# First modulation rows of a transformer layer: fp32 products replaced by split single-pass products with a folding matmul

## The chip, the cores and the metric

The kernel runs on one core of a Trainium2 chip. The time is the device time of one execution in microseconds (us). The engines are TensorE (PE, matmuls; its weight loads are shown apart as PEld), VectorE (DVE), ScalarE (ACT), GpSimd (POOL) and SyncE (SP), whose queue issues the DMA transfers. Each engine works through its instructions in order; semaphores tie them together.

## The reference

One layer of a diffusion backbone works on 1024 latent tokens and 256 context tokens of width 1024. At its start two vectors, `c` for the latent tokens and `c_ctx` for the context tokens, go through silu and a weight matrix of 1024 x 6144. The six pieces of the result shift, scale and gate the tokens later on. The change concerns the first two pieces, shift and scale of the first norm:

```python
mod = jax.nn.silu(c) @ w_mod[l] + b_mod[l]
mod_c = jax.nn.silu(c_ctx)[None, :] @ w_mod[l] + b_mod[l]
sh1, sc1, g1, sh2, sc2, g2 = jnp.split(mod, 6, axis=-1)
sh1c, sc1c, g1c, sh2c, sc2c, g2c = jnp.split(mod_c, 6, axis=-1)
...
h = modulate(rms_norm(x, norm1_w[l]), sh1, sc1)
hc = modulate(rms_norm(ctx, norm1_w[l]), sh1c, sc1c)
```

`h` and `hc` then enter a combined input projection, two token mixers (windowed attention with context keys, and a two-way mLSTM), the merge, and a convolutional feed-forward part. All data is fp32.

## The kernel before

The tokens stand in blocks of 128. Most large products are done in split form: an fp32 operand is taken apart into a high part, which ACT writes as `fp32r` (a format that PE multiplies in a single pass), and a low part, the difference, which DVE writes. The helper is `split_from` (lines 47 to 49); `mm3` (lines 85 to 92) adds up three of the four products of the parts.

`stage_startup` (from line 276) makes the first modulation rows. The silu of both vectors is `sil`, 128 x 8 x 2: for each of 8 blocks `k` of the inner dimension a stationary operand of two columns, one for each vector. The weights come as 16 blocks `wm` of 128 x 1024 (512 KB), 8 for each of two sweeps `i`; a sweep yields half of the channels of shift and scale. For each block two fp32 matmuls of 512 columns add into two PSUM tiles `pm`, of which two partitions are in use (lines 359 to 365). After a sweep, `modulation(i)` (line 320) copies the two rows into `mrow` on DVE and ACT, turns them by 8 transposes into `pmT`, so that channels lie along partitions, and DVE makes `mods` out of that.

With `mods` ACT shifts and scales the turned context (`xct`, line 348) into `hfc` (line 337), and splits it into `hcH` and `hcL`. The first half of the channels is done after sweep 0, the second after sweep 1. The context's keys (`pkc`), values (`pvc`) and mLSTM inputs (`cx`) follow as split products, with the latent tokens' norms, transposes and modulation (`hf`, `hH`, `hL`) in between; from about 106 us on the kernel runs on PE in split products.

The order on each engine is not the order of the code: a scheduler places the instructions, and what is printed below for the order is what comes out of it. The weights of the start share one pool of 11 blocks (`block`, line 285) with the context and latent tokens and the weights `w1b` that follow; a load into a block waits for the last reader of what lay there. SP issues all these loads in one fixed order. The tiles `hT` (8 pairs of `hH` and `hL`, 128 x 1024 each) are first written when the latent tokens are modulated, long after the two sweeps.

Of the kernel before, what the change touches and what calls it, by code (L numbers as in the profile page):

```python
# [8 lines left out]
F32 = mybir.dt.float32  # L9
F32R = mybir.dt.float32r  # L10
AF = mybir.ActivationFunctionType
ALU = mybir.AluOpType
# [4 lines left out]
P = 128  # L17
# [4 lines left out]
KT = D // P  # L22
# [20 lines left out]
def copy_act(nc, out, in_, scale=1.0):  # L43
    nc.scalar.activation(out, in_, AF.Copy, scale=scale)  # L44


def split_from(nc, hi, lo, src, eng="v"):
    copy_act(nc, hi, src)
    (nc.vector if eng == "v" else nc.gpsimd).tensor_tensor(lo, src, hi.bitcast(F32), op=ALU.subtract)  # L49
# [50 lines left out]
def layer_kernel(ctx: ExitStack, tc: tile.TileContext, A: dict, out: bass.AP, dbg=None):  # L100
# [58 lines left out]
    with ExitStack() as st:  # L159
        at = attention_setup(E, st)  # L160
        stage_startup(E, at)
        if "hT" in dbg:
            for k in range(KT):
                nc.sync.dma_start(dbg["hT"][0, k * P : (k + 1) * P], hH[k].bitcast(F32))
                nc.sync.dma_start(dbg["hT"][1, k * P : (k + 1) * P], hL[k].bitcast(F32))
        if dbg.get("stop") != "hT":
            stage_attention(E, st, at)
# [108 lines left out]
def stage_startup(E, at):  # L276
    nc, tc, A, ident, expo, vecT, mods = E.nc, E.tc, E.A, E.ident, E.expo, E.vecT, E.mods
    mm_tile, tp_tile, s_tile, wts = E.mm_tile, E.tp_tile, E.s_tile, E.wts
    H = KT // 2
    with ExitStack() as st:  # L280
        sp = st.enter_context(tc.tile_pool(name="st1", bufs=1, reuse_waits="tile"))
# [3 lines left out]
        def block(name):  # L285
            return xp.tile([P, D], F32, tag="x", name=name)

        rows = sp.tile([P, 2, P], F32, name="vrows")
        nc.sync.dma_start(rows, A["vecs"].rearrange("(a p) c -> p a c", p=P))
        pv = tp_tile("pv")  # L290
        for a in range(2):
            nc.tensor.transpose(pv[:, a * P : (a + 1) * P], rows[:, a], ident)
        nc.vector.tensor_copy(vecT, pv[:, :256])
        sil = E.sil3
        nc.scalar.activation(
            sil.rearrange("p k c -> p c k"), vecT[:, 0:16].rearrange("p (c k) -> p c k", c=2), AF.Silu
        )

        ss = sp.tile([P, NBLK], F32, name="ss")
        rs = sp.tile([P, NBLK], F32, name="rs")  # L300

        def load(i):
            t = block(f"x{i}")
            src = A["ctx"][i * P : (i + 1) * P] if i < NCB else A["x"][(i - NCB) * P : (i - NCB + 1) * P]
            nc.sync.dma_start(t, src)
            return t

        def norm(i, t):
            junk = wp.tile([P, D], F32, tag="junk", name=f"xj{i}", bufs=1)
            nc.scalar.activation(junk, t, AF.Square, accum_out=ss[:, i : i + 1])  # L310
            nc.gpsimd.tensor_scalar(ss[:, i : i + 1], ss[:, i : i + 1], 1.0 / D, EPS, op0=ALU.mult, op1=ALU.add)
            nc.gpsimd.tensor_tensor(rs[:, i : i + 1], ss[:, i : i + 1], expo[:, 0:1], op=ALU.pow)
            nc.vector.tensor_scalar(t, t, rs[:, i : i + 1], None, op0=ALU.mult)


        pm0 = s_tile("pm0")
        pm = [[pm0[:2, 0:512], pm0[:2, 512:1024]], [mm_tile("pm2")[:2], mm_tile("pm3")[:2]]]
        bT = vecT[:, 32:48].rearrange("p (s k) -> p s k", s=2)

        def modulation(i):  # L320
            mrow = sp.tile([P, 1024], F32, name=f"mrow{i}", tag="mrow")[:2]
            nc.vector.tensor_copy(mrow[:, 0:512], pm[i][0])
            copy_act(nc, mrow[:, 512:1024], pm[i][1])
            pT = tp_tile(f"pmT{i}")
            for j in range(8):
                nc.tensor.transpose(pT[:, 2 * j : 2 * j + 2], mrow[:, j * P : (j + 1) * P], ident[:2, :2])
            pTv = pT[:, :16].rearrange("p (s k c) -> p s c k", s=2, c=2)
            ks = slice(H * i, H * i + H)
            for c in (1, 0):
                nc.vector.tensor_tensor(mods[:, 2 + c, ks], pTv[:, 0, c], bT[:, 0, ks], op=ALU.add)  # L330
                nc.vector.scalar_tensor_tensor(mods[:, c, ks], pTv[:, 1, c], 1.0, bT[:, 1, ks], op0=ALU.add, op1=ALU.add)
                nc.vector.tensor_tensor(mods[:, c, ks], mods[:, c, ks], vecT[:, 16 + H * i : 16 + H * i + H], op=ALU.mult)
# [10 lines left out]
        def turn_context(k2):  # L343
            pt = tp_tile(f"xct{k2}")
            for j in range(2):
                for c in range(NCB):
                    k = 2 * k2 + j
                    nc.tensor.transpose(
                        pt[:, (2 * j + c) * P : (2 * j + c + 1) * P], xc[c][:, k * P : (k + 1) * P], ident
                    )  # L350
            return pt

        def context(k2, pt):
            for j in range(2):
                k = 2 * k2 + j
                modulated(1, k, *hc[k], pt[:, j * NCTX : (j + 1) * NCTX], f"c{k}")

        for i in range(2):
            for k in range(KT):
                w = block(f"wm{i}_{k}")  # L360
                nc.sync.dma_start(w, A["w_modA"][i][:, k])
                for n in range(2):
                    nc.tensor.matmul(
                        pm[i][n], sil[:, k], w[:, n * 512 : (n + 1) * 512], start=k == 0, stop=k == KT - 1
                    )
                if i == 0 and k in (3, 4):
                    xc.append(load(k - 3))
            if i == 0:
                modulation(0)
                for c in range(NCB):  # L370
                    norm(c, xc[c])
                for k2 in range(2):
                    context(k2, turn_context(k2))
        at.constants()
        wkc = wts.load(A["w_kc"], 256, block)
        pts = [turn_context(k2) for k2 in (2, 3)]
        modulation(1)
        for k2 in (2, 3):
            context(k2, pts[k2 - 2])
# [77 lines left out]
        for i in range(4):  # L457
# [5 lines left out]
            w = []  # L463
# [1319 lines left out]
```

## Time and profile before

| | |
|---|---|
| median of the runs | 1979.98 us (1974.65, 1979.98, 1980.81) |
| span of the profiled execution | 1981.6 us; the page gives no other time for it |
| POOL busy | 335.9 us (17%) |
| HBM read and written | 197.48 MB and 65.61 MB, 133 GB/s over the span |
| chain that ended last, by engine | PE 78%, DMA 8%, DVE 6%, ACT 4%, issue 2%, POOL 1% |
| transfers `wm` (`in_w_modA`) | 16 of 512 KB, median 7.9 us from issue to landing |

A row of a timeline or of the chain begins with its start and its length in us; "x4" is the number of instructions put together, and a bracket at its end tells how long the engine had been idle and who ended that. A row of a group gives the number of instructions, then the busy time and the mean length of one in ns, then the idle time before them. `L49` is line 49 of the kernel. Names carry no buffer numbers. The length of a matmul includes its way through the array, so matmuls follow each other faster than their lengths say: what one costs in a dense run is the distance of two starts. In rows of stretches the granted clock is a share of PE's full clock.

### The profile page before, as it was taken

How to read it: one execution, taken by the hardware profiler on the slowest of the kernel's cores; microseconds unless marked ns; L12 is line 12 of the kernel's file. 1: busy time of each engine (PE TensorE's matmuls, PEld its weight loads, DVE VectorE, ACT ScalarE, POOL GpSimd, SP SyncE). 2: the span in 40 equal slices, each digit the busy share in tenths (PEclk: the TensorE clock that was granted, in tenths of full speed). 3: DMA queues.
4: the chain of work that ended last, by engine and by line, in shares of the span. 5: the costliest groups of instructions: out<-in, count | busy, mean ns of one | idle time of the engine just before them, and what ended most of it. 6: DMA issues, size and time to landing. Idle time of an engine off the chain costs nothing.

```text
span 1981.6 us, 28514 instructions
## 1 busy us (share of the span) xinstructions
PE 1935.3 (98%) x10108; PEld 1651.5 (83%) x10108; DVE 1357.7 (69%) x2734; ACT 966.8 (49%) x1891; POOL 335.9 (17%) x578
## 2 busy tenths in 40 slices
PE   8999999999999999999999999999999999999999
PEld 3988888888888889898998788787888888888887
DVE  2767877777677555656566256559978988896565
ACT  4845556565556454545445232247544444455441
POOL 1323323333332233333212000010000000000000
PEclk9999999999999999999999999999999999999999
DMA  8731222313222211212107565752235544489651
GB/s 305 229 121 50 82 67 65 93 50 90 62 62 80 63 56 39 78 33 78 33 30 250 192 233 165 273 183 75 107 122 188 190 170 159 181 292 329 232 177 64
DMA packets 124013, 264.94 MB, mean 134 GB/s; under 512 B 13904, under 2 KB 38112, under 8 KB 121056
## 3 DMA queue, kind: packets, MB, share of 16 engines
q1 hardware_dynamic: 116960, 250.55, 37.7%
q10 hardware_dynamic: 6912, 12.59, 1.9%
q8 instruction: 79, 1.29, 0.3%
q14 instruction: 62, 0.51, 0.1%
HBM read 197.48 MB, written 65.61 MB: 133 GB/s over the span
## 4 chain that ended last, share of the span: by engine, by line
PE 78%; DMA 8%; DVE 6%; ACT 4%; issue 2%; POOL 1%; SPq 0%; ACTq 0%; POOLq 0%; DVEq 0%
PE pa L1385 4%; PE pa L1386 4%; PE pa L1387 4%; PE pt L623 3%; PE g L92 3%; PE g L91 2%; PE g L90 2%; PE po L617 2%; PE dx L1385 2%; PE dx L1387 2%; PE dx L1386 2%; PE pb L1385 2%; PE pb L1386 2%; PE pb L1387 2%; PE kv L90 2%
## 5 line engine op out<-in xcount | busy, mean ns | idle before, releaser
L604 POOL TENSOR_SCALAR P<-P,st 128x640 f32<-128x640 f32 (+1 forms) x128 | 111.0, 884 | 268.0 <-DVE st L602 161.1
L595 ACT ACTIVATE P<-P,st 128x640 f32<-128x640 f32 (+1 forms) x128 | 102.5, 801 | 30.4 <-DVE st L591 29.7
L49 DVE TENSOR_TENSOR pl<-pt,ph 128x512 fp32r<-128x512 f32 x152 | 101.6, 687 | 13.9 <-ACT ph L44 12.2
L44 ACT ACTIVATE ph<-pt 128x512 fp32r<-128x512 f32 x152 | 87.6, 596 | 48.0 <-PE pt L623 47.0
L591 DVE CUSTOM_DVE_ANT_0 P<-s,maskA,nsink 128x640 f32<-128x640 f32 (+1 forms) x112 | 103.2, 922 | 11.1 <-PE s L588 8.6
L90 PE MATMUL g<-hH,fh 128*128 128x512 f32 x256 | 103.2, 403 | 0.1
L623 PE MATMUL pt<-ident,P 128*128 128x128 f32 x608 | 98.5, 273 | 3.6 <-POOL P L604 2.9
L92 PE MATMUL g<-hH,fl 128*128 128x512 f32 x256 | 100.7, 393 | 0.7 <-DVE fl L49 0.7
L91 PE MATMUL g<-hL,fh 128*128 128x512 f32 x256 | 100.6, 393 | 0.0
L90 PE MATMUL kv<-w1h,hH 128*128 128x384 f32 x256 | 86.3, 339 | 1.0 <-ACT w1h L44 1.0
L90 PE MATMUL pq<-w1h,hH 128*128 128x384 f32 (+1 forms) x256 | 87.2, 340 | 0.0
L92 PE MATMUL pq<-w1h,hL 128*128 128x384 f32 (+1 forms) x256 | 86.7, 339 | 0.0
L91 PE MATMUL pq<-w1l,hH 128*128 128x384 f32 (+1 forms) x256 | 86.5, 338 | 0.0
L91 PE MATMUL kv<-w1l,hH 128*128 128x384 f32 x256 | 86.4, 338 | 0.0
L92 PE MATMUL kv<-w1h,hL 128*128 128x384 f32 x256 | 86.4, 338 | 0.0
L623 PEld LDWEIGHTS pt<-ident,P 128*128 128x128 f32 x608 | 73.5, 140 | 14.9 <-POOL P L604 7.4
L922 POOL TENSOR_SCALAR kwh<-k,gcall 128x128 fp32r<-128x128 f32 x72 | 34.0, 475 | 227.5 <-PE dC L91 170.6
L90 PE MATMUL mo<-w1h,hH 128*128 128x256 f32 x256 | 72.2, 282 | 0.0
L92 PE MATMUL mo<-w1h,hL 128*128 128x256 f32 x256 | 72.1, 282 | 0.0
L91 PE MATMUL mo<-w1l,hH 128*128 128x256 f32 x256 | 71.9, 281 | 0.0
L49 DVE TENSOR_TENSOR dfl<-drf,dfh 128x512 fp32r<-128x512 f32 x55 | 38.0, 691 | 48.2 <-ACT dfh L44 48.1
L49 DVE TENSOR_TENSOR VL<-kv,VH 128x256 fp32r<-128x256 f32 x32 | 13.6, 424 | 82.1 <-ACT VH L44 81.9
(559 smaller groups left out, 6367.6 us busy)
## 6 DMA issues: line engine op xcount, KB each, us to landing
ur<-in_w_up SPq DMA_DIRECT2D x22, 1024.0 KB, 5.0
wmb<-in_w_modB SPq DMA_DIRECT2D x64, 256.0 KB, 3.0
f_d<-cv SPq DMA_DIRECT2D x22, 512.0 KB, 2.7
wm<-in_w_modA SPq DMA_DIRECT2D x16, 512.0 KB, 7.9
fr<-in_w_g SPq DMA_DIRECT2D x32, 256.0 KB, 3.4
drf<-fs_d SPq DMA_DIRECT2D x15, 512.0 KB, 5.0
drw<-wt_d SPq DMA_DIRECT2D x14, 512.0 KB, 5.6
w1b<-in_w_cx SPq DMA_DIRECT2D x16, 388.0 KB, 4.7
```

Of the source, the lines that this page charges most:

```text
L44: nc.scalar.activation(out, in_, AF.Copy, scale=scale)
L49: (nc.vector if eng == "v" else nc.gpsimd).tensor_tensor(lo, src, hi.bitcast(F32), op=ALU.subtract)
L90: nc.tensor.matmul(ps, lh[:, ls], rh[:, rs], start=start and i == 0, stop=False)
L91: nc.tensor.matmul(ps, lh[:, ls], rl[:, rs], start=False, stop=False)
L92: nc.tensor.matmul(ps, ll[:, ls], rh[:, rs], start=False, stop=stop and i == n - 1)
L591: nc.vector.tensor_tensor_reduce(pm[:, :W], ps[:, off : off + W], mask[:, :W], scale=ss[:, h : h + 1], scalar=nsink[:, hh : hh + 1], op0=A ...
L595: nc.scalar.activation(pm[:, :W], pm[:, :W], AF.Exp, bias=st4[:, h : h + 1], scale=-1.0, accum_out=st4[:, 4 + h : 5 + h])
L604: nc.gpsimd.tensor_scalar(Ps[h][:, :W], Ps[h][:, :W], st4[:, 12 + h : 13 + h], 1.0, op0=ALU.mult, op1=ALU.mult)
L623: nc.tensor.transpose(pt[:, h * P : (h + 1) * P], Ps[h][:, kb * P : (kb + 1) * P], ident)
L1385: nc.tensor.matmul(ps, lh, rh, start=start and i == 0, stop=False, skip_group_check=True)
L1386: nc.tensor.matmul(ps, lh, rl, start=False, stop=False, skip_group_check=True)
L1387: nc.tensor.matmul(ps, ll, rh, start=False, stop=stop and i == n - 1, skip_group_check=True)
```

## The change

The fp32 matmuls of the two sweeps are replaced by split ones. The stationary operand of block `k` becomes 128 columns of fp32r: columns 0 and 1 are the high parts of the two silu vectors, 2 and 3 their low parts, the rest are zeros. It lives in the last tile of `hT`, which POOL fills with zeros first. Each weight block is split by `split_from` into one of the other seven pairs of `hT` tiles, in turn, and each part is multiplied with the whole stationary operand, so that four rows of `pm` hold the products with high and low vectors and all four products of the parts are added up. In `modulation` the four rows are turned and folded to two in one step: a fp32 matmul with a 4 x 2 matrix `fold` (two unit matrices under each other) takes the place of the transpose.

```diff
+        nc.gpsimd.memset(E.hT[KT - 1][1].bitcast(F32), 0.0)
...
+        silS = E.hT[KT - 1][1].rearrange("p (k c) -> p k c", c=P)
+        split_from(nc, silS[:, :, 0:2], silS[:, :, 2:4], sil)
+        fold = sp.tile([4, 2], F32, name="fold")
+        nc.vector.tensor_tensor(fold, ident[:4, 0:2], ident[:4, 2:4], op=ALU.add)
...
-        pm = [[pm0[:2, 0:512], pm0[:2, 512:1024]], [mm_tile("pm2")[:2], mm_tile("pm3")[:2]]]
+        pm = [[pm0[:, 0:512], pm0[:, 512:1024]], [mm_tile("pm2"), mm_tile("pm3")]]
...
-            mrow = sp.tile([P, 1024], F32, name=f"mrow{i}", tag="mrow")[:2]
-            nc.vector.tensor_copy(mrow[:, 0:512], pm[i][0])
-            copy_act(nc, mrow[:, 512:1024], pm[i][1])
+            mrow = sp.tile([P, 1024], F32, name=f"mrow{i}", tag="mrow")[:4]
+            nc.vector.tensor_copy(mrow[:, 0:512], pm[i][0][:4])
+            copy_act(nc, mrow[:, 512:1024], pm[i][1][:4])
             pT = tp_tile(f"pmT{i}")
             for j in range(8):
-                nc.tensor.transpose(pT[:, 2 * j : 2 * j + 2], mrow[:, j * P : (j + 1) * P], ident[:2, :2])
+                nc.tensor.matmul(pT[:, 2 * j : 2 * j + 2], mrow[:, j * P : (j + 1) * P], fold, start=True, stop=True)
...
                 w = block(f"wm{i}_{k}")
                 nc.sync.dma_start(w, A["w_modA"][i][:, k])
-                for n in range(2):
-                    nc.tensor.matmul(
-                        pm[i][n], sil[:, k], w[:, n * 512 : (n + 1) * 512], start=k == 0, stop=k == KT - 1
-                    )
+                hl = E.hT[(i * KT + k) % (KT - 1)]
+                split_from(nc, *hl, w)
+                for p, wp_ in enumerate(hl):
+                    for n in range(2):
+                        nc.tensor.matmul(
+                            pm[i][n], silS[:, k], wp_[:, n * 512 : (n + 1) * 512],
+                            start=k == 0 and p == 0, stop=k == KT - 1 and p == 1,
+                        )
```

The order moves at a few places, all of them before the context's values; behind them every engine has the same instructions in the same order as before, and on SP nothing moves at all.

DVE around the end of the first sweep, before. `x` are the two context blocks being normed, `mrow` the copied rows, `hcL` the low parts of the context.

```order
L313 TENSOR_SCALAR x_189<-x_189,rs 128x1024
L322 COPY mrow_203<-pm_148 2x512
L330 TENSOR_TENSOR mods<-pmT_206,vecT 128x4
L331 SCALAR_TENSOR_TENSOR mods<-pmT_206,vecT 128x4
L330 TENSOR_TENSOR mods<-pmT_206,vecT 128x4
L332 TENSOR_TENSOR mods<-mods,vecT 128x4
L331 SCALAR_TENSOR_TENSOR mods<-pmT_206,vecT 128x4
L332 TENSOR_TENSOR mods<-mods,vecT 128x4
L49 TENSOR_TENSOR hcL_152<-hfc_236,hcH_151 128x256
```

The same place of DVE after; `wm_5` to `wm_7` belong to the first sweep, `wm_0` to `wm_2` here to the second.

```order
L318 TENSOR_SCALAR x_214<-x_214,rs 128x1024
L49 TENSOR_TENSOR hL_99<-wm_5_216,hH_91 128x1024
L49 TENSOR_TENSOR hL_100<-wm_6_224,hH_92 128x1024
L49 TENSOR_TENSOR hL_94<-wm_7_232,hH_86 128x1024
L49 TENSOR_TENSOR hL_95<-wm_0_294,hH_87 128x1024
L327 COPY mrow_240<-pm_153 4x512
L49 TENSOR_TENSOR hL_96<-wm_1_302,hH_88 128x1024
L335 TENSOR_TENSOR mods<-pmT_243,vecT 128x4
```

The subtractions of three blocks of the first sweep stand behind the second norm; one of the second sweep stands ahead of the row copy, and one between that copy and `mods`.

DVE around the end of the second sweep, before (`w1l` are low parts of the context keys' weights):

```order
L49 TENSOR_TENSOR hcL_158<-hfc_253,hcH_157 128x256
L49 TENSOR_TENSOR w1l_294<-w1b_291,w1h_293 128x2x256
L49 TENSOR_TENSOR w1l_300<-w1b_297,w1h_299 128x2x256
L322 COPY mrow_325<-pm_149 2x512
L49 TENSOR_TENSOR w1l_306<-w1b_303,w1h_305 128x2x256
L49 TENSOR_TENSOR w1l_312<-w1b_309,w1h_311 128x2x256
L330 TENSOR_TENSOR mods<-pmT_328,vecT 128x4
```

And after:

```order
L49 TENSOR_TENSOR hcL_163<-hfc_290,hcH_162 128x256
L49 TENSOR_TENSOR hL_98<-wm_3_318,hH_90 128x1024
L49 TENSOR_TENSOR hL_99<-wm_4_326,hH_91 128x1024
L49 TENSOR_TENSOR hL_100<-wm_5_334,hH_92 128x1024
L49 TENSOR_TENSOR hL_94<-wm_6_342,hH_86 128x1024
L49 TENSOR_TENSOR hL_95<-wm_7_350,hH_87 128x1024
L49 TENSOR_TENSOR w1l_363<-w1b_360,w1h_362 128x2x256
L49 TENSOR_TENSOR w1l_369<-w1b_366,w1h_368 128x2x256
L49 TENSOR_TENSOR w1l_375<-w1b_372,w1h_374 128x2x256
L327 COPY mrow_394<-pm_154 4x512
L49 TENSOR_TENSOR w1l_381<-w1b_378,w1h_380 128x2x256
L335 TENSOR_TENSOR mods<-pmT_397,vecT 128x4
```

Five subtractions of weight blocks stand between the first half of the context and the key weights, and three instead of two key weights stand ahead of the row copy. ACT has the five casts at the same place, behind the eight steps of the first half of the context. On PE the 8 transposes of the context's second half stand inside the second sweep and no longer behind it, and 11 matmuls of `pkc` stand between the end of the sweep and the second fold.

## The prediction

> **What bounds the kernel now.** I read the page first, then busy time by stretch over the start, then the chain that ended last, and then single rows for durations.
>
> ```profile
> span 1981.6 us, 28514 instructions
> PE 1935.3 (98%) x10108; PEld 1651.5 (83%) x10108; DVE 1357.7 (69%) x2734; ACT 966.8 (49%) x1891; POOL 335.9 (17%) x578
> ```
>
> TensorE (PE) is the bound of the kernel as a whole. The change touches its first 40 us only, so the question is how much sooner the rest may begin. Columns here: stretch, length, busy time (and count) of PE, weight loads, VectorE (DVE), ScalarE (ACT), POOL, then granted clock, DMA share, GB/s.
>
> ```profile
> 5.79:22.64 16.85, 16.85 (x33) 3.00 (x34) 2.18 (x3) 2.30 (x4) 1.49 (x4) 1.00 1.02 408
> 24.42:38.24 13.82, 13.82 (x33) 2.63 (x32) 4.06 (x12) 5.66 (x12) 0.00 (x0) 1.00 0.82 262
> 40.48:49.45 8.97, 6.53 (x52) 5.86 (x51) 4.60 (x11) 8.32 (x18) 3.06 (x7) 0.99 0.66 234
> 49.45:52.61 3.16, 3.16 (x14) 3.16 (x15) 3.09 (x5) 1.81 (x5) 1.89 (x2) 0.50 0.66 213
> ```
>
> The first two rows are the sweeps: PE busy throughout, DVE and ACT nearly idle. But in the first the DMA is saturated as well (1.02). After them ACT, not PE, is the busy engine (8.32 of 8.97). The chain of waits says the same (start, length, what):
>
> ```profile
> 5.79 16.85 PE pm L363 x32
> 24.49 13.82 PE pm L363 x32
> 38.31 1.02 PE xct L348 x8
> 39.34 0.59 PE pmT L326 x8
> 40.48 1.02 ACT hfc L337 x2
> 48.72 0.69 DVE w1l L49
> 49.45 0.58 PE pvc L91
> 107.21 0.23 PE g L92
> ```
>
> From 40.48 (the first ACT step that needs the second half of the rows) on, the chain runs over ACT, POOL and DVE; only near 106 us does it become the steady PE chain. So my yardstick is that step: what it moves, the end moves, unless something fixed in time stands in between.
>
> **When the weights land.** The loads are issued in an unchanged order. The two context blocks are the 5th and 7th of its 512 KB loads, and ACT starts on each when it lands:
>
> ```profile
> 5.52 0.22 ACT L295 ACTIVATE sil<-vecT 128x16 f32<-128x16 f32 x1 [3.52 <-DVE vecT L293]
> 10.83 1.06 ACT L310 ACTIVATE xj<-x 128x1024 f32<-128x1024 f32 x1 [5.09 <-DMA x<-in_ctx]
> 13.46 1.06 ACT L310 ACTIVATE xj<-x 128x1024 f32<-128x1024 f32 x1 [1.48 <-DMA x<-in_ctx]
> 15.56 0.75 DVE L313 TENSOR_SCALAR x<-x,rs 128x1024 f32<-128x1024 f32 x1 [1.88 <-POOL rs L312]
> ```
>
> (13.46 - 10.83)/2 = 1.315 us a load. The last block of sweep 1 is the 10th: 13.46 + 3 x 1.315 = 17.4. The last of sweep 2 is the 18th: 27.9. No change of arithmetic can make these earlier.
>
> **The price of a block.** Before: 4 fp32 records at 0.43 (13.82/32), 1.73 us. After: 4 single-pass records at 0.23 (the row at 107.21), 0.92, but ahead of them an ACT cast and a DVE subtraction of 128x1024. Both forms exist elsewhere in this kernel; how much successive ones overlap is read from runs of four:
>
> ```profile
> L44 ACT ACTIVATE q1h<-s 128x1024 fp32r<-128x1024 f32 x21 | 22.2, 1057 | 4.1 <-DVE s L1447 3.6 <-issue 0.3
> L49 DVE TENSOR_TENSOR q1l<-s,q1h 128x1024 fp32r<-128x1024 f32 x21 | 25.6, 1218 | 1.8 <-ACT q1h L44 1.8
> 46.64 2.17 ACT L44 ACTIVATE w1h<-w1b 128x512 fp32r<-128x512 f32 x4
> 48.72 2.49 DVE L49 TENSOR_TENSOR w1l<-w1b,w1h 128x512 fp32r<-128x512 f32 x4
> L49 DVE TENSOR_TENSOR w1l<-w1b,w1h 128x512 fp32r<-128x512 f32 x8 | 5.1, 683 | 1.4 <-ACT w1h L44 1.4
> L44 ACT ACTIVATE w1h<-w1b 128x512 fp32r<-128x512 f32 x8 | 4.7, 622 | 3.3 <-DMA w1b<-in_w_kc 3.3
> ```
>
> Four of DVE's take 2.49 against 4 x 0.683, so each next one saves 0.08: a 128x1024 subtraction costs 1.22, then 1.14. For ACT the saving is 0.1: 1.06, then 0.96. **DVE becomes the pace: 1.14 a block, against 0.92 on PE.** All told DVE gets 16 x 1.14 = 18 us of new work in a stretch where it worked little; PE loses 16.85 + 13.82 - 64 x 0.23 = 16 us.
>
> **Sweep 1, as a sum.** DVE is done with the second context block's norm at 15.56 + 0.75 = 16.3. Then come blocks 5, 6 and 7: 1.22 + 2 x 1.14 = 3.5, end 19.8 (ACT has cast block 7 by 17.4 + 1.06 = 18.5, so DVE is later). Two closing matmuls, 0.46: PE is through at 20.3 instead of 22.64. DVE however has the low part of the next sweep's block 0 in front of the copy of the rows (1.14, to 21.0), and the copy takes 0.6 to 0.68:
>
> ```profile
> 21.82 0.68 DVE L322 COPY mrow<-pm 2x512 f32<-2x512 f32 x1 [5.51 <-PE pm L363]
> 24.68 1.02 ACT L337 ACTIVATE hfc<-xct,mods 128x256 f32<-128x256 f32 x2 [1.42 <-DVE mods L331]
> 27.11 0.73 ACT L44 ACTIVATE hcH<-hfc 128x256 fp32r<-128x256 f32 x2
> ```
>
> On PE a matmul on the second sweep's block 1 precedes the fold; ACT makes its high part after its own row copy, so by about 20.3 + 0.6 + 1.06 = 22.0. The fold then takes 0.59 (as the 8 transposes at 39.34) to 1.18: the trace shows each fp32 matmul as two records (32 calls, 64 records), a transpose as one. I take 1.18: end 23.2. From the end of the transposes to the first ACT step the trace has 40.48 - 39.93 = 0.55, so ACT starts on the context at 23.8 rather than 24.68.
>
> **Sweep 2.** The context holds ACT from 24.68 to 27.84 now, 3.16; after, to about 27.0. Five casts (blocks 3 to 7) stand behind it in ACT's queue although their data is there. The first is done at 28.0, DVE follows: 28.0 + 1.22 + 4 x 1.14 = 33.8; PE is through at 34.3 instead of 38.24. DVE next does three weight subtractions (0.61 each, to 35.6) and only then copies the rows (to 36.2). The transposes of the context that now stand at 38.31 lie inside the sweep, so the fold can begin at 36.3 and ends at 37.5; the ACT step begins at **38.0 instead of 40.48: 2.5 us earlier.**
>
> **The small parts.** The fill of 128x1024 on POOL, between nothing and 1.5 us (a 128x640 pass of POOL takes 884 ns), ends before ACT needs it at 6.8. The split of the silu vectors (0.22, as the silu, on each engine) comes while blocks are still landing at 1.315. The fold matrix is one tiny operation. All three: 0, hidden by the wait for loads. The buffers of weights are now freed by DVE's subtraction, not by PE:
>
> ```profile
> L604 POOL TENSOR_SCALAR P<-P,st 128x640 f32<-128x640 f32 (+1 forms) x128 | 111.0, 884 | 268.0 <-DVE st L602 161.1
> 22.68 7.42 SPq L70 DMA_DIRECT2D w1b<-in_w_kc x4
> 31.48 5.48 SPq L305 DMA_DIRECT2D x<-in_x x4
> 37.05 2.10 SPq L70 DMA_DIRECT2D w1b<-in_w_vc x4
> ```
>
> By the sum above DVE frees sweep 1's last buffers from 18.6 and sweep 2's from 21.0 to 33.8, so these loads, queued in order on SP, are issued some 1 to 5 us earlier: no one waits longer for them.
>
> **The clock.** The stretch from 49.45 had a granted clock of 0.50, and the chain shows what that does to one and the same matmul of 256 columns:
>
> ```profile
> 50.25 0.21 PE pvc L90
> 53.08 0.12 PE pvc L92
> ...
> 49.45 0.58 PE L91 MATMUL pvc<-w1l,hcH 128*128 128x256 f32 x1 [1.76 <-DVE w1l L49]
> ```
>
> It came after PE had idled 1.76 us (the last row, of the timeline) and before that had done little but a few transposes. After the change PE idles often, longest from about 25.5 to 28. Half clock for 3.2 us costs sweep 2 about 4 x 0.23 + 0.92 - 1.14 = 0.7 a block for two blocks, of which the later ones win some back; but DVE's row copy waits until 35.6 while PE ends at 34.3, so 1.3 us are covered. Lower end 0, upper end 2.5 (also the 11 matmuls and the fold ahead of the step at half rate); I take 0.
> The Trainium skill ("TensorE: Matmul & The Clock Gate", Part 1) says that one idle window of some 3.4 us puts the array back to half its clock, and that busy time of that length releases it. By that rule sweep 2's idle stretch alone, estimated at 2.5 us, would not throttle and the sum would stay; the trace shows half clock after shorter full idleness with light work around it, so I count on the row.
>
> **Sum.** The profiled execution spans 1981.6, 1.6 above the median of the runs, 1979.98. 2.5 off the median: **1977.5 us**, a ratio of 0.9987. The three runs lie 6 us apart, so about 0.3% (6 us) is what a measurement here tells from nothing.
>
> **Rivals.**
> 1. *The start shrinks to what the loads allow (faster).* Counted on PE alone it would be the 16 us; the loads cap it: 27.9 + 1.06 + 1.22 + 0.46 = 30.6 for the end of sweep 2, 7.6 earlier, and a microsecond of transposes moved inside: about 8.6, 1971. For it: PE is the only busy engine of the sweeps. Against: 11 subtractions and the context stand between 16.3 and 27.9 on DVE, and the rows say 1218 ns. Chance 0.08.
> 2. *The clock stays at half (slower).* If PE's light load never lifts it, sweep 2 takes 5 x 1.84 from 28.0, to 37.2, eleven 256-column matmuls 2.3, the fold 2.4: the step at 42.4, 1.9 late. The 33 matmuls that ran at 0.12 in the pvc group take 3.0 more: 1980 + 4.9 = 1985. It passes 0.3% from the point where the half clock lasts some ten matmuls into the next products (388 columns, by their size about 0.18 more each): 1987. For: the 0.50 row. Against: it was back within 3.2 us of dense work. Chance 0.07.
> 3. *Cast and subtraction don't overlap (slower).* At 1.06 + 1.22 a block instead of 1.14 the eleven blocks whose pace DVE sets cost 11 x 1.1 = 12 more, less the 2.5: 1989. Against: each has its own buffers, and q1h and q1l show DVE 1.8 us idle in all 21. Chance 0.06.
> 4. *The gain is lost on the way* from 40.48 to 106, at a load or a half-clock stretch that falls otherwise: 1980, no change to be measured. Chance 0.19.
>
> The forecast keeps 0.60. Faster 0.08, slower 0.13, same 0.79. The range goes from 1973.5 (0.59 for each fold, and the lower runs' level) to 1984, which takes in most of rival 2.
>
> **What would show it.** Right: subtractions of 128x1024 back to back on DVE near 1.14 in sweep 2; PE ending it near 34.3, with waits on DVE; the second set of context steps on ACT at 38.0; the same pattern behind it, shifted. Wrong: matmuls of 512 columns at 0.43 past 30 us, DVE waiting for ACT in every block, or a fold above 1.2.

## The result, and the profile after

The changed kernel takes 1985.21 us in the median (1982.62 to 1986.91) beside 1980.07 for the kernel before in the same measurement: a ratio of 1.0029, 95% interval 1.0018 to 1.0041. It is slower, by 5 to 6 us; 2.5 us less had been forecast. Single executions far off the rest, one of `e6_extra_instr` (4915 us) and one of `e9_turn_bias` (5637 us), are in no ratio below (without them the medians there are 1986.31 and 1984.89).

The heads of the two profiles don't show this: the profiled execution after has a span of 1981.3 us, that of before 1981.6. Single executions scatter by 6 us before and by 4 us after even in this small measurement, so the pair of traces tells where the steps went, and only the medians tell what they cost.

```profile
span 1981.3 us, 28599 instructions
PE 1929.8 (97%) x10124; PEld 1662.6 (84%) x10124; DVE 1376.9 (69%) x2752; ACT 983.1 (50%) x1908; POOL 336.9 (17%) x579
```

DVE and ACT got 19 and 16 us more work. PE is busy for 5.5 us less, and yet the end is not earlier. The chain of waits over the startup (start, length, what):

```profile
16.58 1.23 DVE hL L49
17.86 3.02 PE pm L371 x10
...
21.39 1.05 ACT hH L44
22.49 0.50 PE pm L371
22.98 1.87 PE pmT L331 x16
24.85 0.60 PE xct L353 x4
25.48 1.02 ACT hfc L342 x2
...
28.63 0.95 ACT hH L44
29.61 1.24 DVE hL L49
30.89 5.29 PE pm L371 x18
36.19 0.60 ACT mrow L44
...
38.41 1.87 PE pmT L331 x16
```

The sweeps did become short and hang on ACT and DVE, as forecast. But each fold (`pmT`) stands in the chain with 1.87 us and 16 records, where a turn of before had 8 records and 0.59. The prediction's yardstick, the second context step on ACT, comes at 40.78 us; it was 40.48 before, and 38.0 was forecast. In the timelines of DVE and ACT of the changed kernel:

```profile
29.61 5.76 DVE L49 TENSOR_TENSOR hL<-wm,hH 128x1024 fp32r<-128x1024 f32 x5 [0.49 <-ACT hH L44]
37.09 0.67 DVE L327 COPY mrow<-pm 4x512 f32<-4x512 f32 x1
40.78 1.02 ACT L342 ACTIVATE hfc<-xct,mods 128x256 f32<-128x256 f32 x2 [2.44 <-DVE mods L337]
```

Busy time by stretch (stretch, length, PE, weight loads, DVE, ACT, POOL, granted clock, DMA share, GB/s) shows a second thing. In this execution PE ran at half clock from 40.7 and again from 51.0 us (and once more from 109 us), for 3.4 us each, the second time under the dense matmuls of the context values:

```profile
40.70:44.10 3.40, 3.40 (x19) 3.40 (x18) 2.19 (x8) 3.32 (x9) 0.00 (x0) 0.50 0.62 249
51.00:54.40 3.40, 3.40 (x18) 3.40 (x17) 3.33 (x6) 1.69 (x3) 1.55 (x2) 0.50 0.95 275
```

### The profile page after: what moved, and what is told of

The parts are those of the page before. It is cut to its first block, busy times and chain, and to the rows that moved or that the text cites. A ratio compares the mean times of both kernels' runs of the same rounds, so it can differ in the third digit from the quotient of the medians.

```text
span 1981.3 us, 28599 instructions
## 1 busy us (share of the span) xinstructions
PE 1929.8 (97%) x10124; PEld 1662.6 (84%) x10124; DVE 1376.9 (69%) x2752; ACT 983.1 (50%) x1908; POOL 336.9 (17%) x579
## 4 chain that ended last, share of the span: by engine, by line
PE 82%; DVE 6%; DMA 6%; ACT 4%; issue 1%; POOL 1%; SPq 0%; ACTq 0%; POOLq 0%; DVEq 0%
PE pa L1394 4%; PE pa L1395 4%; PE pa L1396 4%; PE pt L632 3%; PE g L92 3%; PE g L91 3%; PE g L90 2%; PE po L626 2%; PE dx L1394 2%; PE dx L1396 2%; PE dx L1395 2%; PE pb L1394 2%; PE pb L1395 2%; PE pb L1396 2%; PE kv L90 2%; PE kv L91 2%
## 5 line engine op out<-in xcount | busy, mean ns | idle before, releaser
L44 ACT ACTIVATE ph<-pt 128x512 fp32r<-128x512 f32 x152 | 87.6, 596 | 47.7 <-PE pt L632 46.8
```

## The experiments

Three suspects: the fold, the granted clock (theory E), and the place of TensorE's instruction loads (theory C). Below, "step" is the start of the second context step on ACT in the profiled execution; where "1.0005" or the like stands with an interval, it is the ratio to the kernel before in the same measurement. The runs came from three chips; the kernel before had nearly the same median on each (1980.9 to 1981.2 us). Both kernels were run again first, as a scale for the profiled executions.

**Both kernels again (e1_before, e2_after).** No edit.

> The kernel before, once more, beside itself. Theory A (the profile of before fell into a slow execution of its kernel, so the two traces can't be subtracted at their end): its span here is 1973 to 1979, and its first ACT step with the second half of the rows stands at 40.5 again, within 0.3. Theory B (the traces are typical, and the loss arises only in the start): the span is 1981 to 1982 again. Under A the mean granted clock of the runs is 0.998 with two short half-clock stretches; if the clock differs from run to run as it does after the change (0.995 to 0.997), the clock alone can't explain the loss.

> The changed kernel, once more, on the same chip as the kernel before. Both theories: 3 to 7 us over before. Theory A (the start loses under 1 us, and the rest follows from half-clock stretches that the new idle times of PE bring on): the trace again has half-clock stretches near 41, 51 and 109 us, and from 112 to 130 us its matmuls stand some 3 to 4 us behind those of before. Theory B (the start loses all of it): they stand 5 us or more behind already at 60 us.

Before: 1982.6 us, 1.0005 [0.9994, 1.0017], step at 39.44. After: 1986.43 us, 1.0028 [1.0016, 1.0040], step at 41.98. So the result repeats, and the step of one kernel moves by about 1 us from one execution to another: 40.48 in the trace that the prediction worked from was a late one. The microsecond arose at the start. In that trace the first seven records of sweep 1 stand 0.81 to 0.85 us apart, as at half clock, and the rest 0.43; in e1_before only the first five do, and sweep 1 takes 15.97 us instead of 16.85 (15.62 in e4_fp32_turn below). The clock column reads 1.00 there in both. On this chip the change made the step 2.5 us later, not earlier.

**The fold's form alone, in the kernel before (e4_fp32_turn).** The fp32 matmul takes the place of the transpose; nothing else of the change is there.

```diff
-                nc.tensor.transpose(pT[:, 2 * j : 2 * j + 2], mrow[:, j * P : (j + 1) * P], ident[:2, :2])
+                nc.tensor.matmul(pT[:, 2 * j : 2 * j + 2], mrow[:, j * P : (j + 1) * P], ident[:2, :2], start=True, stop=True)
```

> The kernel before with one part of the change alone: the two rows are turned by fp32 matmuls with a 2 x 2 unit matrix, 16 records, instead of 8 transposes; the sweeps stay in fp32. Theory A (the turn by a true fp32 matmul is what eats the start's gain, about 1.3 us each, and both lie on the chain): 8 turns take 1.9 instead of 0.6 us, the context steps of ACT start 1.3 and then 2.6 us later, 41.8 for the first sweep's shift alone or 43.1 with both; the time is 1 to 3 us over before. Rival (the turns are hidden by other work): the step stays at 40.5 and the time within 0.5 us.

1985.71 us, 1.0025 [1.0016, 1.0034]: nearly as slow as the whole change, without its split sweeps. Sweep 1 and the second turn in the chain of waits of the kernel before (run again), and the second turn in that of this one:

```profile
5.64 15.97 PE pm L363 x32
...
37.28 1.02 PE xct L348 x8
38.30 0.59 PE pmT L326 x8
39.44 1.02 ACT hfc L337 x2
```

```profile
38.41 1.02 PE xct L348 x8
39.43 1.89 PE pmT L326 x16
41.86 1.02 ACT hfc L337 x2
```

The two turns put the step 2.4 us later. A small fp32 matmul is two records and two weight loads, and 16 records take 1.89 us in the chain, 0.118 each; a transpose is one record, 0.074 each (0.59/8). The trace of before did hold such matmuls, in a later modulation row, though not as turns. Four fp32 matmuls with one column each are 8 records in 0.95 us there, which would have put 16 records at 1.9:

```profile
177.86 0.95 PE L224 MATMUL ms<-expo,macc 128*128 128x1 f32 x8
```

**The fold in one record, in the changed kernel (e5_fold_single).** Row copies and fold matrix in fp32r, so the low part of the turned rows is left out.

```diff
-        fold = sp.tile([4, 2], F32, name="fold")
+        fold = sp.tile([4, 2], F32R, name="fold")
...
-            mrow = sp.tile([P, 1024], F32, name=f"mrow{i}", tag="mrow")[:4]
+            mrow = sp.tile([P, 1024], F32R, name=f"mrow{i}", tag="mrow")[:4]
```

> The changed kernel with rows and folding matrix in fp32r, so that the folding matmuls are single-pass records; the order on all engines is that of the changed kernel. Left out is the low part of the turned rows: the modulation is rounded there. Theory A (fold's price is its two passes): 8 folds take 0.6 to 1.0 instead of 1.87, the second ACT step starts at 39.0 to 39.8 instead of 40.8, and the time is 1 to 2 us under the changed kernel's. Rival (the price lies in the weight load of a 4 x 128 operand, whatever the type): the fold still takes over 1.5 and nothing moves.

1983.09 us, 1.0005 [0.9996, 1.0013]. The chain of waits:

```profile
22.58 0.98 PE pmT L331 x8
24.41 1.02 ACT hfc L342 x2
37.34 0.99 PE pmT L331 x8
38.82 1.02 ACT hfc L342 x2
```

The step is 3.2 us earlier than in the changed kernel on the same chip (38.82, 41.98), and the loss is gone. With the rows rounded, taking away the fold's second record thus takes away the larger part of what the change lost. But 0.6 us of gain at the step (39.44 to 38.82) shows as no gain in the time.

**Is DVE the pace (e8_no_sub)?** As e5_fold_single, without the subtraction; both matmul pairs take the rounded weights. The weights' low parts are left out, and the high parts are counted twice, so the modulation rows come out about doubled; the instructions are as long.

```diff
-                split_from(nc, *hl, w)
+                copy_act(nc, hl[0], w)
+                hl = (hl[0], hl[0])
```

> As e5_fold_single, and the subtraction of the weights' low parts left out: both matmul pairs of a block take the rounded weights, so the low parts are left out of the result and DVE has nothing to do in the sweeps, while TensorE and ACT do as much as before. Theory D (DVE's 1.15 us a block sets the pace of the sweeps, as predicted): the last matmul of either sweep comes one subtraction earlier and sweep 2 saves some 0.2 us a block more, so the second context step is at 36.5 to 37.3 instead of 38.8 us, and the time 1.5 to 2.5 us under e5_fold_single (about 1981). Rival (TensorE's matmuls, 0.29 us each in the chain, set the pace): the second context step at 38.2 to 38.8, and the time as e5_fold_single.

```profile
26.64 5.94 PE L372 MATMUL pm<-hH,hL 128*128 128x512 f32 x24 [1.40 <-ACT hH L44]
36.20 1.02 ACT L342 ACTIVATE hfc<-xct,mods 128x256 f32<-128x256 f32 x2 [1.44 <-DVE mods L337]
```

1980.57 us, 0.9993 [0.9983, 1.0003], step at 36.20: 2.6 us earlier than with the subtraction. By the ratios the time is 2.4 us less, though their intervals overlap. Theory D, DVE as the pace, holds at the step, with somewhat more than it gave. The scheduler also moved three subtractions of key weights behind the row copy. But from the end of PE's sweep 2 to the step it is 3.7 us with the subtraction (35.11 to 38.82) and 3.8 without (32.36 to 36.20), so the gain arose in the sweeps. Left to ACT, PE runs the 24 matmuls of sweep 2 at 5.94/24 = 0.25 each.

**More instructions on TensorE (e6_extra_instr, e7_single_extra, then e13_single_hidden, e14_before_hidden).** In the traces with the two-record turn, PE is 1 to 1.6 us later, against the same matmuls of the kernel before (run again), from 149 us on; in those without it, not. They hold 32 more instructions of PE. Eight small fp32 matmuls (32 instructions) were put at the start of the kernel before, and of the kernel with the single fold:

```diff
             nc.tensor.transpose(pv[:, a * P : (a + 1) * P], rows[:, a], ident)
+        for j in range(8):
+            nc.tensor.matmul(pv[:, 256 + 2 * j : 258 + 2 * j], rows[:2, 0], ident[:2, :2], start=True, stop=True)
```

> The kernel before, with eight small fp32 matmuls of two rows more behind the first two transposes, into columns of their PSUM tile that nothing reads, while TensorE waits for the first weights. They cost the chain nothing: TensorE has 4 us to spare there. They add to TensorE's program as many instructions (16 weight loads, 16 matmul records) as the turn by fp32 matmuls adds, and so move every later instruction fetch of TensorE earlier in the program. Theory C (the part of the loss that comes after 48 us is the place of the fetches): the second context step stays at 39.4 us, and the offset against the kernel before then jumps by 0.9 to 1.5 us near 149 us, where the loads of w1r are waited for, and by 1.0 to 1.7 us near 540 us; the run is 1 to 3 us slower (ratio 1.0005 to 1.0015). Rival (the loss is the longer chain of the startup and what the clock makes of it): no jumps, 1.0000 within 0.0006.

> The changed kernel with the fold in one record (as in e5_fold_single: copied rows and fold matrix rounded to fp32r, so the low part of the turned rows is left out), with the same eight small fp32 matmuls behind the first two transposes. Against e5_fold_single its chain is the same and its instruction count on TensorE is that of the changed kernel. Theory C: 1 to 3 us slower than e5_fold_single (1983.1), so 1984 to 1986, with jumps near 149 and 540 us. Rival: as e5_fold_single, 1983 within 1.

1986.41 us, 1.0019 [1.0006, 1.0031], and 1985.07 us, 1.0016 [1.0004, 1.0028]. Both tell less than they were meant to. The matmuls were no free work: the copy of `vecT` waited for them, since they write into its tile, and so early a record took 0.22 us (3.52/16), twice what it takes later on, as at half clock:

```profile
4.38 3.52 PE pv L294 x16
7.92 0.44 DVE vecT L295
```

The steps came at 42.92 (3.5 us late) and 40.40 (1.6 late), which is by itself most of what the times show. The jump at 149 us is there in both, 1.2 and 1.5 us. The test was made again with sixteen transposes in a tile of their own, ahead of the first weights:

```diff
+        more = E.fl_tile("more")
+        for j in range(16):
+            nc.tensor.transpose(more[:, 2 * j : 2 * j + 2], rows[:2, 0], ident[:2, :2])
```

> As e5_fold_single, with sixteen fp32 transposes of two rows (16 weight loads, 16 matmul records) into an unused PSUM tile, at the start, where TensorE waits for the first split weights, and in a tile that nobody waits for: e7_single_extra without the delay that its extra matmuls put on the first rows. Its chain should be that of e5_fold_single to 0.2 us up to 100 us. Theory C (32 more instructions on TensorE move its instruction fetches so that one meets the loads of w1r near 149 us): the offset against e5_fold_single jumps by 1.0 to 1.6 us there and the run is 1 to 2 us slower, 1983 to 1984 in the mean. Rival (the jump went with the later chain): no jump, and 1982 within 0.7.

> The kernel before with the same sixteen transposes at the same place. TensorE idles there for 1.5 us; at the clock of the first microseconds the sixteen may take 2.3 us and make the first weights wait for up to 1 us, which is then seen at the second context step (39.4 to 40.4 us). Theory C: beyond that delay a jump of 1.0 to 1.6 us near 149 us, the time 1 to 2.5 us over the kernel before. Rival: no jump, the time over the kernel before by the startup's delay alone, 0 to 1 us.

On the single fold the step stayed (38.93 against 38.82), on the kernel before it is 1.5 us late (40.97). Both traces have the jump at 149 us: 1.2 and 1.6 us. What PE lacks there is a weight block: ACT waits for the load of `w1r`. The load's time from issue to landing near that place, first with the single fold alone, then with the sixteen transposes:

```profile
L70 SPq DMA_DIRECT2D w1r<-in_w_att x2: 384/384/385, 143.2 to 144.8; - x2
DMA to landing us min/median/max: 3.3/3.5/3.8
```

```profile
L70 SPq DMA_DIRECT2D w1r<-in_w_att x2: 384/386/388, 146.7 to 148.4; - x2
DMA to landing us min/median/max: 4.0/4.4/4.8
```

In the first trace a load of PE's instructions starts at 149.1, when these blocks have landed; in the second at 149.4, in the middle of their flight. In all eight traces with 16 or more additional records on PE the jump is there (0.8 to 1.6 us), in none of the others; the profiled execution at a clock of 0.938 (below) doesn't tell. The chain was also later in those eight, by 2.9 us or more at 148 us against at most 2.3 in the others. But the late traces among the others (the first trace of before by 2.1, e8_no_sub by 2.3) have the instruction load as much later, 4.2 to 4.5 us behind the issue of the second block; in the eight it starts between 0.4 us ahead of that issue and 1.3 behind it. So its place goes with the number of instructions, not with the delay. That the instruction load itself delays the blocks fits but wasn't separated from the instructions. And in the time it is not to be seen: 1981.68 us, 1.0005 [0.9993, 1.0018], beside 1.0005 without them; on the kernel before 1983.62 us, 1.0010 [0.9998, 1.0023], of which the late step explains 1 to 1.5 us. Theory C holds for the place; that it costs time isn't shown, and intervals of 2.4 to 2.6 us to either side could hide a jump of 1.2.

**The clock (e11_single_busy, e12_after_busy).** Each execution has its mean granted clock on record. Of 113 executions of the kernel before, those at 0.999 took 1978.6 us in the mean (23 of them), those at 0.998 1980.7 (40), at 0.997 1982.7 (39), at 0.996 1984.1 (9): some 2 us for each 0.001. One stretch of 3.41 us at half clock is 3.41 x 0.5/1980 = 0.0009 of the mean clock and, where PE is the bound, 3.41 x 0.5 = 1.7 us. So a part of the scatter is a count of such stretches: in the kernel before the clock goes with about half of the variance (0.48 of it), while among the executions of e5_fold_single and e8_no_sub alone no slope shows. The kernel before has 0.9977 in the mean, the changed one 0.9960 and 0.9949 in its two measurements: two or three stretches more. Two fp32 matmuls (four records, 1.7 us) were put where PE waits for the weights of the context values, in the kernel with the single fold and in the changed kernel. No order of another engine changed.

```diff
+                if i == 0 and k == 0:
+                    busy = E.fl_tile("busy")
+                    for r in range(2):
+                        nc.tensor.matmul(
+                            busy, hc[KT - 1][0][:, 0:P].bitcast(F32), vecT[:, None, :].to_broadcast([P, 2, 256]), start=True, stop=True
+                        )
```

> As e5_fold_single (fold in one record, its rows rounded to fp32r), with two fp32 matmuls of 128x512 more (some 1.7 us of TensorE) between the block of context keys and that of context values, into a PSUM tile that nothing reads yet. There TensorE stood idle for 3 of the 4 us from 44 to 48 us in e5_fold_single, and a stretch of 3.41 us at half clock followed at 47.7 us, under the 48 matmuls of the values. No other engine's order changes. Theory E (idle TensorE in the startup brings a half-clock stretch onto the dense work that follows, 1.7 us each, and the split sweeps bring more of them than the kernel before has): the stretch at 47 to 51 us is gone, the mean clock of the executions rises from 0.9958 to about 0.9967 and the time falls by 1 to 2 us against e5_fold_single (1981.9 in the mean), to 1980 to 1981. Rival (the matmuls after 47 us wait for loads and casts anyway, and the clock costs nothing there): as e5_fold_single within 0.7 us.

> The changed kernel whole, with the same two fp32 matmuls at the same place. Theory E: the half-clock stretch at 51 us is gone, the mean clock rises by 0.001 or more from 0.995 to 0.996, and the time falls by 1.5 to 3 us, to 1982.5 to 1984. Rival: 1985 to 1986.5 as before.

The changed kernel without and with them, by stretch (columns as above):

```profile
47.70:51.10 3.40, 0.93 (x4) 0.50 (x5) 1.57 (x5) 3.40 (x7) 1.91 (x4) 1.00 0.01 2
51.10:54.50 3.40, 3.40 (x16) 3.40 (x17) 3.33 (x6) 2.29 (x5) 1.65 (x2) 0.50 0.70 212
```

```profile
47.70:51.10 3.40, 2.20 (x9) 0.88 (x7) 1.54 (x5) 3.40 (x7) 1.91 (x4) 1.00 0.01 2
51.10:54.50 3.40, 3.30 (x27) 3.30 (x28) 3.33 (x7) 2.83 (x6) 1.65 (x2) 1.00 0.72 212
```

With 2.20 us of PE's 3.40 busy instead of 0.93, the next stretch runs at full clock and does 27 matmuls instead of 16. Useless work made the kernel faster: 1982.79 us, 1.0005 [0.9995, 1.0015], where the changed kernel had 1.0028, at the same step (42.05 and 41.98). Its mean clock rose from 0.9949 to 0.9971. With the single fold: 1979.67 us, 0.9992 [0.9981, 1.0003], where 1.0005 stood without, clock from 0.9958 to 0.9977, and the stretch at 47.7 us gone likewise. Without them (the stretch at 23.8 us, which stays in both, is shown too), and with them:

```profile
20.40:23.80 3.40, 2.97 (x17) 1.85 (x16) 2.48 (x6) 2.48 (x3) 0.00 (x0) 1.00 1.03 412
23.80:27.20 3.40, 3.40 (x14) 2.81 (x12) 2.26 (x8) 2.79 (x8) 0.00 (x0) 0.50 0.91 351
44.30:47.70 3.40, 0.67 (x4) 0.47 (x4) 1.72 (x5) 3.40 (x9) 2.01 (x5) 1.00 0.00 0
47.70:51.10 3.40, 3.31 (x15) 3.31 (x16) 3.40 (x7) 1.39 (x3) 0.96 (x2) 0.50 0.70 225
```

```profile
44.40:47.80 3.40, 1.90 (x9) 1.18 (x10) 1.72 (x4) 3.40 (x8) 2.40 (x6) 1.00 0.00 0
47.80:51.20 3.40, 3.40 (x31) 3.40 (x30) 3.40 (x6) 1.94 (x4) 0.58 (x1) 1.00 0.90 248
```

Theory E holds for the changed kernel, whose two intervals just don't overlap; with the single fold the time moved the same way, but the intervals overlap. One trace each is thin evidence for the stretch itself: of the eleven traces without the pair (that at 0.938 aside) ten have such a stretch, starting between 46.1 and 51.3 us, and e1_before, without any edit, hasn't. In both kernels the mean clock rose by 0.002, two stretches and not only the one at which the edit aimed. Beyond the startup the traces differ in such stretches even between two executions of one kernel (after: at 109 us; e2_after: at 734 and 1119), so which others went, no run shows. Nor was the pair of matmuls tried in the kernel before, which may gain by it too.

The traces also say which stretches the change added, and it is not the one that was filled: the first trace of before has it too, from 49.3 us, behind 3.41 us with 1.10 us of work on PE. The five traces with fp32 sweeps have 1, 0, 1, 1 and 1 half-clock stretches up to 60 us, all near 50 us. The three with the two-record fold have 2, 4 and 3; new are those from 23.8 us (two in a row, in e2_after and e12_after_busy) and from 40.7 to 40.9 us (in all three). With the single fold and split sweeps as in the changed kernel, four traces (e5, e13, e7 and e11) have 2, 2, 1 and 1, and none from 40.7. What precedes the new ones is no idle time: PE is busy for 2.98 of 3.41 us ahead of 23.8 (e2_after), and for all of them ahead of 40.7 (changed kernel, columns as above):

```profile
37.31:40.72 3.41, 3.41 (x30) 3.26 (x29) 1.46 (x7) 1.03 (x2) 0.74 (x2) 1.00 0.87 262
40.73:44.14 3.41, 3.41 (x18) 3.41 (x18) 2.20 (x8) 3.36 (x9) 0.00 (x0) 0.50 0.61 244
```

A fold stands ahead of each, and no trace with the single fold has the one from 40.7. So a part of the clock's price hangs on the fold, as far as seven traces tell. Why PE's work there doesn't keep the clock up stays open.

**A whole version without the fold (e9_turn_bias).** Four rows turned by transposes, the parts added on DVE.

```diff
-                nc.tensor.matmul(pT[:, 2 * j : 2 * j + 2], mrow[:, j * P : (j + 1) * P], fold, start=True, stop=True)
...
+                nc.tensor.transpose(pT[:, 4 * j : 4 * j + 4], mrow[:, j * P : (j + 1) * P], ident[:4, :4])
...
+            lob = sp.tile([P, 2, 2, H], F32, name=f"lob{i}")
+            nc.vector.tensor_tensor(lob, p4[:, 1], bT[:, None, :, ks].to_broadcast([P, 2, 2, H]), op=ALU.add)
...
-                nc.vector.tensor_tensor(mods[:, 2 + c, ks], pTv[:, 0, c], bT[:, 0, ks], op=ALU.add)
+                nc.vector.tensor_tensor(mods[:, 2 + c, ks], pTv[:, 0, c], lob[:, c, 0], op=ALU.add)
```

> The changed kernel with the four rows turned by transposes again (one record each), and the two parts summed on DVE: low part plus bias in one 128x16 operation for both vectors, to which the six operations of before then add the high part. Nothing is left out. The turn should cost 0.6 us instead of 1.9 and DVE 0.1 to 0.2 us more. Theory (the fold by fp32 matmuls is what made the change slow): the second context step at 38.6 to 39.2 and the time 1981.5 to 1983.5, so 1.5 to 3 us under the changed kernel and level with the kernel before. Rival (the split itself loses): 1985 or more. A scheduler orders the code by its own estimate, and some instructions of the block keys trade places; up to 1 us either way may come from that.

The step is where it was expected, at 38.49, and the time is not: 1985.41 us, 1.0021 [1.0010, 1.0031]. The chain of waits:

```profile
37.11 0.68 PE pmT L329 x8
38.49 1.02 ACT hfc L343 x2
```

Apart from the profiled execution, whose clock was 0.938, its mean clock was 0.9953, 0.0024 under that of the kernel before: by the 2 us for 0.001 that is 4.8 us, more than the gain at the step. The scheduler also moved the subtractions of the weights and the transposes of `x` in it, and the run doesn't tell the two apart. So one thing stays open: with one record a turn and nothing left out the kernel is nearly as slow as the changed one, though its step and clock are about those of the single fold (38.82, 0.9958), which was level with the kernel before.

**The runs side by side.** The difference to the kernel before (ratio x 1980), against a sum of two things: the step, less 39.96 (the mean of the two profiled executions of before), and 2 us for each 0.001 of mean clock under 0.9977.

| kernel | step us | mean clock | sum us | measured us |
|---|---|---|---|---|
| e1_before | 39.44 | 0.9975 | -0.5 + 0.4 = -0.1 | 1.0 |
| after | 40.78 | 0.9960 | 0.8 + 3.4 = 4.2 | 5.7 |
| e2_after | 41.98 | 0.9949 | 2.0 + 5.6 = 7.6 | 5.5 |
| e4_fp32_turn | 41.86 | 0.9969 | 1.9 + 1.6 = 3.5 | 5.0 |
| e5_fold_single | 38.82 | 0.9958 | -1.1 + 3.8 = 2.7 | 1.0 |
| e6_extra_instr | 42.92 | 0.9975 | 3.0 + 0.4 = 3.4 | 3.8 |
| e7_single_extra | 40.40 | 0.9965 | 0.4 + 2.4 = 2.8 | 3.2 |
| e8_no_sub | 36.20 | 0.9966 | -3.8 + 2.2 = -1.6 | -1.4 |
| e9_turn_bias | 38.49 | 0.9953 | -1.5 + 4.8 = 3.3 | 4.2 |
| e11_single_busy | 38.45 | 0.9977 | -1.5 + 0 = -1.5 | -1.6 |
| e12_after_busy | 42.05 | 0.9971 | 2.1 + 1.2 = 3.3 | 1.0 |
| e13_single_hidden | 38.93 | 0.9966 | -1.0 + 2.2 = 1.2 | 1.0 |
| e14_before_hidden | 40.97 | 0.9974 | 1.0 + 0.6 = 1.6 | 2.0 |

The sum comes within 2.3 us of each, and the measured ones have intervals of 1.6 to 2.6 us to either side. Over all rows it misses by 1.2 us (root mean square); the step alone misses by 2.8 and the clock alone by 2.1. The step is that of one execution, the clock a mean over all. The sum counts twice a half-clock stretch that has already made the step late, as those at 23.8 and 40.9 us in the changed kernel's second run.

## Why the prediction was wrong, point by point

Two terms of its sum failed: the fold, taken as 1.18 us where it took 1.87 and more, and the clock, taken as 0 where the mean clock fell by 0.0017 to 0.0028.

- **DVE as the pace, right.** Five subtractions took 5.76 us (1.22 + 4 x 1.14 = 5.78 forecast); DVE was through with sweep 1 at 16.58 + 4.68 = 21.26 (21.0). Without the subtraction the step came 2.6 us earlier.
- **Where the first fold begins, 1 us too early.** The step "until about 22.0" counted ACT's cast of block 1 but not the matmul behind it, and PE ended sweep 1 at 20.9, not 20.3. The chain has ACT's cast at 21.39, PE's matmul at 22.49, the fold at 22.98.
- **The fold, the step that failed.** It was taken as 1.18 us, the row of 8 transposes doubled, and 0.59 to 1.18 given as its bounds. It took 1.87 twice, and 2.57 and 2.11 in the run again, where the clock was half from 23.8 and from 40.9. Two records were counted rightly, but a record of a small fp32 matmul takes 0.117 to 0.118 us of the chain and a record of a transpose 0.074. So 1.18 was no upper bound: it had the nearest row for one size and took it for another form, while the rows `ms` at 177.86 us had the form itself (8 records in 0.95). The prediction's own sign of error, "a fold above 1.2", came true.
- **The second fold, 0.7 us longer and behind a queue.** The row copy was to end at 36.2 and ended at 37.76, for the first turn's lateness went through ACT's casts (28.52 instead of 27.0) and so through DVE. The fold began only at 38.41, since PE stood in matmuls of the context keys, which were ready ahead of it. At the step this made 40.78 of 38.0: 1.0 from the first fold's start, 0.7 from either fold and some 0.5 from the queue, of which 0.1 was won back in between.
- **The clock, taken at 0.** The bounds were 0 and 2.5 us, with the wait for DVE's row copy as cover in sweep 2. In the first trace of the changed kernel no half clock fell into sweep 2; in the second it did (23.8 to 30.6 us), and the step came 1.2 us later (41.98, 40.78), so the cover was not whole. The whole price was beyond the bound: 0.0017 to 0.0028 of mean clock, 3.4 to 5.6 us. Rival 4 had a half-clock stretch that eats the gain on the way; it ate more than the gain. The row that the prediction counted on, half clock from 49.45 us behind a nearly idle PE, is not what the change added: the new stretches start at 23.8 and 40.7 us, behind a busy PE with a fold on it. The Trainium skill ("TensorE: Matmul & The Clock Gate", Part 1) has it that a free-running window of some 3.4 us is watched and that an idle one halves the clock. The trace agrees in the length (3.41 us) but not in "idle": half clock also followed stretches with 0.67, 0.93 and (20.4 to 23.8 us, single fold) 2.97 us of 3.40 busy, and one with PE busy throughout (37.31 to 40.72 us, changed kernel).
- **The yardstick, half right.** What moves the step moves the time (the table), but the clock moves it as much, and one trace of before, a late one, couldn't show it: its step was 1 us later than that of the next execution. Measured from that other trace, 38.0 would have been 1.4 us of gain and not 2.5. The prediction put the long first sweep beside a saturated DMA (1.02); the spacing of its matmuls, 0.85 us up to 11.7 us and 0.43 from there on, accounts for the length.
- **The sum of the miss.** With the fold in one record and PE kept busy the ratio is 0.9992 [0.9981, 1.0003], -1.6 us; 2.5 less had been forecast. So the two terms can account for the difference between forecast and result within what can be measured. It is an account for rounded rows and added work, though, and e9_turn_bias, without either, doesn't reach it.

## What to carry to other kernels

Price a new instruction form by a row of that form, searched for in the whole trace, or measure it; doubling the nearest form is an estimate and not a bound, above all where the instruction stands alone in a chain. Work taken off PE in a phase that waits for other engines can bring its clock down for the work that follows, as it did here: look at the 3.4 us ahead of each stretch at half clock, and where PE waits there, consider filling them. A busy share alone doesn't say what the clock will do. Where executions scatter, sort them by mean granted clock before a trace is compared with another.

## What was not expected of the hardware

- About half of the scatter of the kernel before goes with the mean granted clock, 2 us for 0.001; one half-clock stretch of 3.41 us is 0.0009 of it.
- Half clock can follow 3.41 us in which PE was busy throughout (37.31 to 40.72 us in the changed kernel).
- Four records of useless matmuls in an idle stretch made the changed kernel faster, by some 4.6 us as the ratios have it (1.0028 to 1.0005, each uncertain by 2 us or more).
- A small fp32 matmul costs PE 0.118 us a record and two records, whether it folds 4 rows (16 in 1.87 us) or turns 2 (16 in 1.89); in fp32r a record takes about as long (8 in 0.98), but is one.
- With 32 more instructions in the first 42 us of PE's program, PE waits 0.8 to 1.6 us longer near 149 us, for a weight block, in every trace that has them and that can tell.
